# Mixer A's head columns stored from pairs of tiles, and the bias tables in 18 steps on GpSimd

## The chip, the cores and the metric

The kernel runs on 1 core of one Trainium2 chip. The metric is the device time of one execution in microseconds (us); the time before is the median of three runs. The profile is of one further execution of the same program on the same core.

## The reference

One layer of a hybrid decoder, batch 1, 2048 positions, width 1024, float32. What is computed, cut to what this case touches:

```
h    = rmsnorm(x, g_attn)
proj = h @ w_in + b_in                      # qa | ka | va | qb | kb | vb
qa, ka = rope(qa), rope(ka)                 # mixer A: 8 query heads, 2 key heads, 64 wide
oa   = banded attention(qa, ka, va), window 128, with sinks
ob   = dilated attention(qb, kb, vb), branches (128,1), (512,4), (2048,16),
       logits + rel_table[t5_bucket(distance)]        # one bias table per head of mixer B
x    = x + concat(rmsnorm(oa), rmsnorm(ob)) @ w_o
x    = x + SwiGLU feed-forward(rmsnorm(x));  return rmsnorm(x)
```

Each float32 product is made of three products of rounded halves: a tensor is split into a rounded high part and the remainder ("high and low").

## The kernel before

The program is built through a layer that puts the instructions of each engine into an order of its own: it takes the program as written, follows dependences and buffers, and may move an instruction ahead of others on its engine. Each engine then works its list strictly in order, so an instruction that waits holds all behind it. All loads and stores spoken of here go through the list of SyncE (SP) and one DMA queue.

Function `project` makes `h` (kept in SBUF as `hh`, `hl`) and v, and then works in two stages.

**The rotary stage** makes qa and ka. There are 20 tiles, numbered 0 to 19 here: for each block of 128 output columns, in the order c = 4 (the two key heads), 0, 1, 2, 3 (two query heads each), four tiles t = 0 to 3 of 512 positions. For one tile:

- `rotated`: `gemm` (L175) sums 24 matmuls into a PSUM buffer `acc` (pool `ps2`, 8 buffers). ScalarE (ACT) and VectorE (DVE) copy two quarters each, swapped, into `t1` (L297, L299); VectorE multiplies by cosine and sine (`t2`, L301; `t1`, L302); GpSimd (POOL) adds them into `t2` (L303). `t1` has 2 buffers, `t2` has 4.
- `parted`: ScalarE casts `t2` into the high part of `hia` (L312) and VectorE subtracts for the low part (L313). `hia` holds one column block of 2048 positions and has 1 buffer. It runs two tiles late: after tile n is rotated, tile n - 2 is parted. After t = 3 the block is stored by two DMAs of 1 MB (`store_heads`, L181): kA for c = 4, then four stores of qA. The next block's first cast can start only when that store has landed.
- The weights of the next block but one are loaded at t = 1 (`load_w`, L163, raw buffer 1) and split by ScalarE (L165) and VectorE (L167, `wl`).

**The bias tables** are made beside it, in the same loop, by the closure that `bias_tables` returns: after tiles 2 to 9 `rows(h)` for the 8 heads (one VectorE operation `lw`, L397, three matmuls `accb` into the same PSUM pool, L400, three ScalarE copies `lt`, L402, 2 buffers, three stores into the scratch `Ls`, L403), after tiles 10 to 17 `table(h)`: loads of `Ls` into `tt`, `n4` and four quarters of `n1` (L407, L409, L412; one buffer each), two VectorE copies that put them into `tt` (L413, L414), and a store of `tt` (L416, `Ts`). The layer brings many of these forward.

**The next stage** starts with tiles 20 to 23 of mixer B's projection (`proj_b`, first weights `C_QB`), whose results `hi` go out to qB, and then mixer A's attention units: logits `s` (L449) from `ka` and `qa`, which are loaded from the stored kA and qA (L549, L557). The list of SyncE holds the last qA store between the loads of `ka`.

Of the kernel before, what the change touches and what calls it, by code (L numbers as in the profile page):

```python
# [10 lines left out]
F32 = mybir.dt.float32  # L11
# [6 lines left out]
P = 128  # L18
# [3 lines left out]
NH = 8  # L22
# [125 lines left out]
def project(tc, es, ident, half, x, g_attn, w_in, b_in, sinks, rel, rope, mask_a, onehot, sc):  # L148
# [129 lines left out]
    with ExitStack() as ex:  # L278
# [27 lines left out]
        def parted(c, t, t2):  # L306

            if t == 0:
                his[c] = rp.tile([P, 2, S], F32R, tag="hi", name="hia", bufs=1)
            hi = his[c]  # L310
            hj = [hi[:, u].rearrange("p (j r a) -> p r j a", j=16, r=16)[:, 4 * t:4 * t + 4] for u in range(2)]
            nc.scalar.copy(hj[0], t2)  # L312
            nc.vector.tensor_sub(hj[1], t2, hj[0].bitcast(F32))  # L313
            if t == NT - 1:
                store_heads(sc.qA if c < 4 else sc.kA, 2 * c if c < 4 else 0, hi, slice(0, S))
# [4 lines left out]
        for n, (c, t) in enumerate(seq):  # L320
            t2 = rotated(c, t, w[c])
            if t == 1 and n + 3 < len(seq):
                cn = seq[n + 3][0]
                w[cn] = load_w(cn * P)
            behind.append((c, t, t2))
            if len(behind) > 2:
                parted(*behind.pop(0))
            if 0 <= n - 2 < 2 * NH:
                bias((n - 2) // NH, (n - 2) % NH)
# [4 lines left out]
    with ExitStack() as ex:  # L334
# [3 lines left out]
        w = {}  # L338

        def proj_b(todo, ps=ps, tag="mm"):  # L340
            for c0, c, t in todo:
                if t == 0:
                    w[c0] = load_w(c0 + c * P)
# [24 lines left out]
def bias_tables(tc, es, ps, rel, onehot, sc):  # L368
# [26 lines left out]
    def rows(h):  # L395
        lw = bw.tile([P, P], F32R, tag="lw", name="lw")
        nc.vector.tensor_scalar(out=lw, in0=ones, scalar1=rhi[:, h:h + 1].bitcast(F32), scalar2=None, op0=ALU.mult)  # L397
        for b in range(3):
            acc = ps.tile([P, 384], F32, tag="mm", name="accb")
            nc.tensor.matmul(acc, lw, ohr[:, b, :], start=True, stop=True)  # L400
            lt = bw.tile([P, 384], F32, tag="lt", name="lt")
            nc.scalar.copy(lt, acc)  # L402
            nc.sync.dma_start(sc.L[h, b], lt)  # L403

    def table(h):
# [7 lines left out]
        nc.vector.tensor_copy(tt[:, 128:384].rearrange("p (c i) -> p c i", c=4), n4.rearrange("p (i c) -> p c i", c=4))  # L413
        nc.vector.tensor_copy(tt[:, 384:640].rearrange("p (g c a) -> p g c a", g=4, c=4),  # L414
# [3 lines left out]
    return lambda step, h: (rows, table)[step](h)  # L418
# [898 lines left out]
```

## Time and profile before

| | |
|---|---|
| median of 3 runs | 2417.63 us (2417.11 to 2417.86) |
| the profiled execution's own time | 2418.66 us |
| its span in the trace | 2416.9 us |
| TensorE (PE) busy | 2295.9 us, 95% of the span |
| VectorE / ScalarE / GpSimd busy | 1601.3 / 1056.2 / 466.5 us |
| mean granted TensorE clock | 0.979 |
| rotary stage, first matmul to first logits of mixer A | 146.69 to 318.65 us |

The span runs from the first to the last instruction on the core; the execution's own time has some 1.8 us around it. A row of the timeline has the start, the time (in us), the engine, line, operation, output<-input and count, and in brackets how long the engine had sat idle and what ended that. In a row of a wait table stand who waited for whom, the total, how often, and the longest.

### The profile page before, as it was taken

What the parts mean: (1) busy time and instruction counts of PE and PEld (TensorE: products, weight loads), DVE (VectorE), ACT (ScalarE), POOL (GpSimd) and SP (SyncE); (2) the same over time, 40 slices, a digit from 0 to 9 for tenths busy, and PEclk for the clock granted to TensorE, in tenths of its full rate; (3) what the DMA queues carried; (4) which work ended last, traced back from release to release, by engine and by line L of the source; (5) the groups of instructions that cost most, each with busy time, mean ns of one, the idle gap of its engine ahead of it and who ended that gap; (6) DMA issues with size and microseconds to landing.
All of it is one profiled execution on the core that took longest, in us unless ns stands there. A gap on an engine that the chain in (4) does not pass through costs nothing.

```text
span 2416.9 us, 33849 instructions
## 1 busy us (share of the span) xinstructions
PE 2295.9 (95%) x11765; PEld 1953.6 (81%) x11765; DVE 1601.3 (66%) x3151; ACT 1056.2 (44%) x2371; POOL 466.5 (19%) x418
## 2 busy tenths in 40 slices
PE   7998799998999989897999999999999999999998
PEld 7986678887999878786788888778888878888887
DVE  5335644446999977658876776796676746657555
ACT  5323245553988873325323323342323325444442
POOL 2321211112111010014132332423232331000000
PEclk9998999998999989998999999999999999999999
DMA  7656576659898697855545444343233329768651
GB/s 220 211 172 195 142 190 177 165 143 258 203 221 211 166 269 193 257 165 193 195 152 175 160 150 166 123 143 101 96 114 100 105 82 397 263 195 290 201 191 70
DMA packets 280091, 436.20 MB, mean 180 GB/s; under 512 B 24224, under 2 KB 152864, under 8 KB 273136
## 3 DMA queue, kind: packets, MB, share of 16 engines
q1 hardware_dynamic: 273600, 419.21, 56.4%
q0 software_dynamic: 3728, 10.30, 1.5%
q10 hardware_dynamic: 2592, 4.52, 0.7%
q8 instruction: 93, 1.52, 0.3%
q14 instruction: 78, 0.64, 0.1%
HBM read 286.50 MB, written 147.46 MB: 180 GB/s over the span
## 4 chain that ended last, share of the span: by engine, by line
PE 51%; DVE 5%; DMA 3%; issue 1%; POOL 0%; ACT 0%; DVEq 0%; POOLq 0%; SPq 0%; ACTq 0%
PE bY L1245 7%; PE Yu L1051 7%; PE Yg L1051 6%; PE bZ L1245 5%; PE bX L1245 5%; PE Zu L1051 4%; PE Xu L1051 4%; PE Xg L1051 4%; PE Zg L1051 4%; PE acco L913 3%; DMA ob<-oB 1%; DVE wl L1018 1%; DMA ob<-oA 1%; DVE xs L935 1%; DMA hraw<-hT 0%
## 5 line engine op out<-in xcount | busy, mean ns | idle before, releaser
L1198 DVE TENSOR_TENSOR o<-r,o 128x1024 fp32r<-128x1024 f32 x154 | 190.5, 1243 | 133.0 <-ACT o L1197 124.6
L1197 ACT CAST o<-r 128x1024 fp32r<-128x1024 f32 x154 | 162.2, 1054 | 227.0 <-DMA r<-in_w_down_dram 61.2
L1016 ACT CAST wh<-T 128x512 fp32r<-128x512 f32 x176 | 107.6, 621 | 247.7 <-PE Yu L1051 78.9
L1145 POOL TENSOR_TENSOR c<-c,c 128x512 f32<-128x512 f32 x66 | 104.3, 1580 | 570.1 <-DVE c L1069 390.7
L496 DVE TENSOR_TENSOR hl<-pt,hl 128x512 fp32r<-128x512 f32 (+1 forms) x224 | 145.5, 657 | 78.4 <-ACT hl L495 77.5
L471 ACT ACTIVATE p<-t,m 128x256 f32<-128x256 f32 (+1 forms) x384 | 177.2, 479 | 16.2 <-DVE m L696 16.2
L175 PE MATMUL acc<-hh,wh 128*128 128x512 f32 x416 | 168.0, 404 | 14.8 <-DVE t L301 13.7
L1245 PE MATMUL bY<-o 128*128 128x512 f32 x792 | 180.5, 389 | 0.0
L1245 PEld LDWEIGHTS bY<-o 128*128 128x128 f32 x792 | 148.6, 188 | 30.9
L913 PE MATMUL acco<-woh,oT 128*128 128x512 f32 x512 | 163.6, 397 | 3.8 <-ACT oT L884 3.4
L175 PE MATMUL acc<-hh,wl 128*128 128x512 f32 x416 | 167.1, 402 | 0.0
L175 PE MATMUL acc<-hl,wh 128*128 128x512 f32 x416 | 166.7, 401 | 0.0
L1018 DVE TENSOR_TENSOR wl<-T,wh 128x512 fp32r<-128x512 f32 x176 | 155.1, 891 | 0.3
L514 PE MATMUL o<-hl,v 128*128 128x128 f32 (+1 forms) x816 | 140.7, 293 | 7.3 <-DVE hl L496 6.0
L495 ACT CAST hl<-pt 128x512 fp32r<-128x512 f32 (+1 forms) x224 | 125.2, 568 | 44.6 <-PE pt L490 43.9
L490 PE MATMUL pt<-ident,p 128*128 128x128 f32 x848 | 135.4, 283 | 3.9 <-DVE hl L496 2.1
L449 PE MATMUL s<-k,q 128*128 128x256 f32 (+1 forms) x768 | 122.5, 292 | 10.1 <-DVE nm L453 6.0
L1245 PE MATMUL bX<-o 128*128 128x512 f32 x528 | 120.6, 389 | 1.1 <-DVE o L1198 1.1
L514 PEld LDWEIGHTS o<-hl,v 128*128 128x128 f32 x816 | 111.3, 193 | 12.0 <-DVE hl L496 9.3
L1245 PE MATMUL bZ<-o 128*128 128x512 f32 x528 | 120.3, 389 | 0.0
L913 PEld LDWEIGHTS acco<-woh,oT 128*128 128x128 f32 x512 | 97.0, 190 | 25.6 <-ACT oT L884 4.1
L1245 PEld LDWEIGHTS bX<-o 128*128 128x128 f32 x528 | 99.0, 188 | 22.1 <-DVE o L1198 1.5
(465 smaller groups left out, 5803.6 us busy)
## 6 DMA issues: line engine op xcount, KB each, us to landing
r<-actS SPq DMA_DIRECT2D x154, 256.0 KB
actS<-c SPq DMA_DIRECT2D x128, 256.0 KB
wraw_g<-in_w_gate_dram SPq DMA_DIRECT2D x44, 512.0 KB
wraw_u<-in_w_up_dram SPq DMA_DIRECT2D x44, 512.0 KB
r<-wT SPq DMA_DIRECT2D x88, 256.0 KB
r<-in_w_down_dram SPq DMA_DIRECT2D x66, 256.0 KB
k<-kB SPq DMA_DIRECT2D x32, 512.0 KB
draw<-in_w_down_dram SPq DMA_DIRECT2D x22, 512.0 KB
```

Source lines behind the costliest of these rows:

```text
L175: nc.tensor.matmul(acc, a[:, k, :], h[t][:, k, :], start=(n == 0), stop=(n == 3 * KC - 1))
L471: nc.scalar.activation(b["pv"](p[:, i, :n]), b["tv"](b["t"]), AF.Exp, scale=-1.0, bias=nm[:, c:c + 1], accum_out=l[:, c:c + 1])
L490: nc.tensor.transpose(pt[:, sl, :], p[:, i, hfn * P:(hfn + 1) * P], ident)
L495: nc.scalar.copy(hi, pt[:, a:z, :])
L496: nc.vector.tensor_sub(lo, pt[:, a:z, :], hi.bitcast(F32))
L514: nc.tensor.matmul(out, v[:, vi, :], mov, start=(first and n == 1), stop=(last and n == 2 * len(jobs)))
L913: nc.tensor.matmul(acc, oT[kk // 2][:, kk % 2, a, i * P:(i + 1) * P], b[:, kk, :], start=(n == 0), stop=(n == 11))
L1018: nc.vector.tensor_sub(lo, src, hi.bitcast(F32))
L1051: nc.tensor.matmul(bank, a[:, k], b[:, k], start=(first and m == 0), stop=(m == 11), skip_group_check=not first)
L1197: nc.scalar.copy(o[:, 0], r)
L1198: V.tensor_sub(o[:, 1], r, o[:, 0].bitcast(F32))
L1245: nc.tensor.matmul(bank[i], o[:, u, 0, i * P:(i + 1) * P], o[:, v, 1, :], start=(first and j == 0 and m == 0), stop=(j == NP - 1 and m == ...
```

## The change

Three things, all in `project` and `bias_tables`:

- `parted` no longer follows two tiles behind. After a tile with t = 3 the block's tiles t = 0 and 1 are parted, after the next block's t = 0 its tiles t = 2 and 3. Both instructions are marked so that the layer keeps them where the program has them. What is left after tile 19 is parted at the end.
- The bias work is cut into 18 steps, one after each tile from 2 to 19: two pieces (one matmul, copy and store each) per step in the first 12, from step 2 on a `load(h)` in each even step and a `table(h)` in each odd one. The two copies into `tt` are on GpSimd.
- The weights of mixer B's first tile are loaded after tile 17, in the loop of the rotary stage.

```diff
-            nc.scalar.copy(hj[0], t2)
-            nc.vector.tensor_sub(hj[1], t2, hj[0].bitcast(F32))
+            tc.keep_in_program_order(nc.scalar.copy(hj[0], t2))
+            tc.keep_in_program_order(nc.vector.tensor_sub(hj[1], t2, hj[0].bitcast(F32)))
...
+            elif t == 1:
+                w_next = load_w(C_QB)
             behind.append((c, t, t2))
-            if len(behind) > 2:
-                parted(*behind.pop(0))
-            if 0 <= n - 2 < 2 * NH:
-                bias((n - 2) // NH, (n - 2) % NH)
+            if t in (0, 3):
+                for x_ in [x_ for x_ in behind if x_[1] in ((2, 3) if t == 0 else (0, 1))]:
+                    parted(*x_)
+                    del behind[[y[:2] for y in behind].index(x_[:2])]
+            if n >= 2:
+                bias(n - 2)
...
-        w = {}
+        w = {C_QB: w_next}
...
-                if t == 0:
+                if t == 0 and (c0, c) != (C_QB, 0):
                     w[c0] = load_w(c0 + c * P)
...
+    def piece(h, b):
+        if b == 0:
+            lws[h] = rows(h)
+        acc = ps.tile([P, 384], F32, tag="mm", name="accb")
+        nc.tensor.matmul(acc, lws[h], ohr[:, b, :], start=True, stop=True)
+        lt = bw.tile([P, 384], F32, tag="lt", name="lt")
+        nc.scalar.copy(lt, acc)
+        nc.sync.dma_start(sc.L[h, b], lt)
...
+    def table(h):
+        tt, n4, n1 = raws[h]
-        nc.vector.tensor_copy(tt[:, 128:384].rearrange("p (c i) -> p c i", c=4), n4.rearrange("p (i c) -> p c i", c=4))
-        nc.vector.tensor_copy(tt[:, 384:640].rearrange("p (g c a) -> p g c a", g=4, c=4),
+        nc.gpsimd.tensor_copy(tt[:, 128:384].rearrange("p (c i) -> p c i", c=4), n4.rearrange("p (i c) -> p c i", c=4))
+        nc.gpsimd.tensor_copy(tt[:, 384:640].rearrange("p (g c a) -> p g c a", g=4, c=4),
                               n1.rearrange("p (a c g) -> p g c a", g=4, c=4))
         nc.sync.dma_start(sc.T[h], tt)
...
+    def bias(step):
+        for n in (2 * step, 2 * step + 1):
+            if n < 3 * NH:
+                piece(n // 3, n % 3)
+        if step >= 2:
+            (table if step % 2 else load)(step // 2 - 1)
```

After the rotary stage, from tile 20 on, every engine's list is the same as before. Where the order moved, at three places:

ScalarE before, around the change from block c = 1 to c = 2 (tiles 12 and 13 of block 2 are t_2274 and t_2322, tiles 14 and 15 are t_2378 and t_2427; COPY t_ is L297 for the tile whose `t1` it names, in the order 12 to 17):

```order
L297 COPY t_2317<-acc 32x512 x2
L312 CAST hia<-t_2274 128x4x16x8
L312 CAST hia<-t_2322 128x4x16x8
L297 COPY t_2373<-acc 32x512 x2
L165 CAST wh_2667<-raw_2665 128x1024
L297 COPY t_2422<-acc 32x512
L312 CAST hia<-t_2378 128x4x16x8
L297 COPY t_2422<-acc 32x512
L297 COPY t_2470<-acc 32x512
L312 CAST hia<-t_2427 128x4x16x8
```

and ScalarE in the change, the same tiles (12 to 15 are t_2276, t_2337, t_2390, t_2433):

```order
L297 COPY t_2332<-acc 32x512 x2
L297 COPY t_2385<-acc 32x512 x2
L165 CAST wh_2530<-raw_2528 128x1024
L297 COPY t_2428<-acc 32x512 x2
L313 CAST hia<-t_2276 128x4x16x8
L313 CAST hia<-t_2337 128x4x16x8
L297 COPY t_2470<-acc 32x512 x2
L313 CAST hia<-t_2390 128x4x16x8
L313 CAST hia<-t_2433 128x4x16x8
```

The casts of a block's first two tiles, which wait for the store of the block before, moved behind the copies of its other two tiles; the casts of these follow one tile later.

GpSimd in the change, around tables 6 and 7 (L427, L428 are the copies; t_2276 to t_2475 are the additions of tiles 12 to 16; before, this list holds the additions alone):

```order
L303 TENSOR_TENSOR t_2276<-t_2276,t_2271 128x512
L427 COPY tt<-n_2487 128x256
L428 COPY tt<-n_2489 128x256
L303 TENSOR_TENSOR t_2337<-t_2337,t_2332 128x512
L303 TENSOR_TENSOR t_2390<-t_2390,t_2385 128x512
L427 COPY tt<-n_2573 128x256
L428 COPY tt<-n_2575 128x256
L303 TENSOR_TENSOR t_2433<-t_2433,t_2428 128x512
L303 TENSOR_TENSOR t_2475<-t_2475,t_2470 128x512
```

The addition of tile 15 now stands behind both copies of the last table.

SyncE in the change, from the store of block c = 1 to that of c = 2 (L413 stores pieces, L417, L419, L422 load the table, L430 stores it, raw_2999 are weights):

```order
L181 DMA qA<-hia 64x2x2048 x2
L413 DMA Ls<-lt 128x384 x2
L417 DMA tt<-Ls 128x128
L419 DMA n_2573<-Ls 128x1x256
L422 DMA n_2575<-Ls 32x1x256
L430 DMA Ts<-tt 128x640
L422 DMA n_2575<-Ls 32x1x256 x3
L417 DMA tt<-Ls 128x128
L163 DMA raw_2999<-in_w_in_dram 128x8x128
L430 DMA Ts<-tt 128x640
L581 DMA qa<-qA 128x2x512 x2
L181 DMA qA<-hia 64x2x2048 x2
```

The last table's loads stand behind the store of block 1, and two loads of `qa` (L581, 512 KB each) directly ahead of the store of block 2; before, there was one table less behind that store.

## Rows read from the trace of the kernel before

**Rows 1.** Busy time of each engine by stretch of the span: the stretch and its length, then busy us and instructions of PE, PEld, DVE, ACT and POOL, the granted share of TensorE's clock, the DMA share and GB/s.

```profile
188.00:213.00 25.00, 17.76 (x52) 13.45 (x53) 13.96 (x23) 10.15 (x19) 3.85 (x3) 0.73 0.73 197
213.00:274.00 61.00, 61.00 (x272) 50.64 (x271) 34.65 (x52) 19.21 (x34) 11.85 (x8) 1.00 0.67 184
274.00:319.00 45.00, 26.68 (x102) 21.02 (x101) 19.15 (x28) 10.91 (x18) 7.88 (x5) 0.85 0.60 143
319.00:560.00 241.00, 239.51 (x1399) 209.83 (x1399) 112.82 (x334) 131.72 (x359) 34.68 (x56) 0.99 0.61 167
```

**Rows 2.** Waits of PE between 150 and 340 us: who waited for whom, us in total, times, the longest.

```profile
PE acc L175 <- DVE t L301: 13.7, 2, 10.0
PE accb L400 <- ACT lt L402: 6.5, 3, 2.5
PE s L449 <- DMA ka<-kA: 4.6, 1, 4.6
```

**Rows 3.** Timeline of PE: the first matmul of tiles 0, 19, 20 and 22, and the first logits.

```profile
146.69 0.50 PE L175 MATMUL acc<-hh,wh 128*128 128x512 f32 x1 [0.65 <-DVE vt L245]
...
268.75 0.39 PE L175 MATMUL acc<-hh,wh 128*128 128x512 f32 x1
...
284.39 0.80 PE L175 MATMUL acc<-hh,wh 128*128 128x512 f32 x1 [10.04 <-DVE t L301]
...
301.18 0.50 PE L175 MATMUL acc<-hh,wh 128*128 128x512 f32 x1 [3.67 <-DVE t L301]
...
318.65 1.35 PE L449 MATMUL s<-ka,qa 128*128 128x128 f32 x7 [4.60 <-DMA ka<-kA]
```

**Rows 4.** Timeline of the DMA issues of SyncE: the five stores of a column block (kA, then four of qA), and the two loads of `qa`.

```profile
187.62 1.33 SPq L181 DMA_DIRECT2D kA<-hia  x2
...
222.03 1.48 SPq L181 DMA_DIRECT2D qA<-hia  x2
...
253.24 1.27 SPq L181 DMA_DIRECT2D qA<-hia  x2
...
267.16 2.37 SPq L557 DMA_DIRECT2D qa<-qA  x2
...
279.43 1.29 SPq L181 DMA_DIRECT2D qA<-hia  x2
...
305.68 1.27 SPq L181 DMA_DIRECT2D qA<-hia  x2
```

**Rows 5.** Timeline of ACT: the four casts that a store had held.

```profile
200.60 0.62 ACT L312 CAST hia<-t 128x512 fp32r<-128x512 f32 x1 [6.76 <-DMA kA<-hia]
...
234.87 1.15 ACT L312 CAST hia<-t 128x512 fp32r<-128x512 f32 x2 [6.29 <-DMA qA<-hia]
...
265.40 1.14 ACT L312 CAST hia<-t 128x512 fp32r<-128x512 f32 x2 [6.66 <-DMA qA<-hia]
...
291.27 1.14 ACT L312 CAST hia<-t 128x512 fp32r<-128x512 f32 x2 [7.71 <-DMA qA<-hia]
```

**Rows 6.** Waits of DVE and of ACT between 150 and 340 us (columns as in rows 2).

```profile
DVE hia L313 <- ACT hia L312: 21.7, 6, 6.2
...
DVE tt L414 <- DMA n<-Ls: 10.9, 5, 5.5
...
DVE tt L413 <- DMA Ts<-tt: 5.8, 4, 2.9
...
ACT lt L402 <- DMA Ls<-lt: 23.5, 11, 5.5
```

**Rows 7.** Timeline of DVE: the first product (L301) of tiles 15, 16 and 17, where nothing but the work itself holds a tile; and a subtraction for the low part (L313).

```profile
275.16 0.75 DVE L301 SCALAR_TENSOR_TENSOR t<-acc,bcol,tab 128x512 f32<-128x512 f32 x1
...
278.71 0.69 DVE L313 TENSOR_TENSOR hia<-t,hia 128x512 fp32r<-128x512 f32 x1
279.43 0.75 DVE L301 SCALAR_TENSOR_TENSOR t<-acc,bcol,tab 128x512 f32<-128x512 f32 x1
...
283.59 0.75 DVE L301 SCALAR_TENSOR_TENSOR t<-acc,bcol,tab 128x512 f32<-128x512 f32 x1 [0.64 <-ACT t L297]
```

**Rows 8.** Round trips over DRAM, from the timelines of SyncE, ACT and DVE, in order of time: a store of two pieces and the copy that waited for its buffer; a table's store and the load that waited for it; the last quarter of `n1` and the copy that read it.

```profile
186.20 0.88 SPq L403 DMA_DIRECT2D Ls<-lt  x2
...
188.44 0.48 ACT L402 COPY lt<-accb 128x384 f32<-128x384 f32 x1 [1.02 <-DMA Ls<-lt]
...
210.75 0.31 SPq L416 DMA_DIRECT2D Ts<-tt  x1
...
213.70 0.43 SPq L407 DMA_DIRECT2D tt<-Ls  x1
...
240.96 0.61 SPq L412 DMA_DIRECT2D n<-Ls  x1
...
243.96 0.38 DVE L414 COPY tt<-n 128x256 f32<-128x256 f32 x1
```

**Rows 9.** GpSimd and VectorE at the same moment, from their timelines, in order of time: an addition, a table copy of VectorE that started beside it, and an addition with a split of weights beside it.

```profile
240.64 1.29 POOL L303 TENSOR_TENSOR t<-t,t 128x512 f32<-128x512 f32 x1 [9.16 <-DVE t L302]
240.67 1.52 DVE L413 COPY tt<-n 128x256 f32<-128x256 f32 x1 [0.20 <-DMA Ts<-tt]
...
270.92 2.83 POOL L303 TENSOR_TENSOR t<-t,t 128x512 f32<-128x512 f32 x1 [9.29 <-DVE t L302]
271.40 1.20 DVE L167 TENSOR_TENSOR wl<-raw,wh 128x1024 fp32r<-128x1024 f32 x1
```

More of the change, by code (lines that the diff above doesn't have):

```diff
@@ L397, in rows, with load @@
         nc.vector.tensor_scalar(out=lw, in0=ones, scalar1=rhi[:, h:h + 1].bitcast(F32), scalar2=None, op0=ALU.mult)
[L398 to L405, printed above, removed]
+        return lw
+    def piece(h, b):
[6 more added lines that the diff above has]
+        nc.sync.dma_start(sc.L[h, b], lt)
+    def load(h):
         tt = bw.tile([P, 640], F32, tag="tt", name="tt", bufs=1)
@@ L412, in table @@
             nc.sync.dma_start(n1[g * 32:(g + 1) * 32], skew(h, 2, [(4, 4), (16, 8)], 127 + (W - 1) * g, 2 * P))
-        nc.vector.tensor_copy(tt[:, 128:384].rearrange("p (c i) -> p c i", c=4), n4.rearrange("p (i c) -> p c i", c=4))
-        nc.vector.tensor_copy(tt[:, 384:640].rearrange("p (g c a) -> p g c a", g=4, c=4),
+        raws[h] = tt, n4, n1
+    def table(h):
+        tt, n4, n1 = raws[h]
+        nc.gpsimd.tensor_copy(tt[:, 128:384].rearrange("p (c i) -> p c i", c=4), n4.rearrange("p (i c) -> p c i", c=4))
+        nc.gpsimd.tensor_copy(tt[:, 384:640].rearrange("p (g c a) -> p g c a", g=4, c=4),
                               n1.rearrange("p (a c g) -> p g c a", g=4, c=4))
         nc.sync.dma_start(sc.T[h], tt)
-    return lambda step, h: (rows, table)[step](h)
+    lws, raws = {}, {}
+    def bias(step):
[4 more added lines that the diff above has]
+            (table if step % 2 else load)(step // 2 - 1)
+    return bias
 ident_f = lambda ap: ap
```

## The prediction

> **What bounds the kernel now.** I read the stretches first. From 213 to 274 us and from 319 us on TensorE has no gap; the change touches the stage up to 319 us alone, so what this stage gives back comes off the whole, and that is the first thing to see [rows 1]. The stage's losses lie in two stretches: from 188 to 213 us TensorE is busy for 17.8 of 25 us at a granted clock of 0.73, from 274 to 319 for 26.7 of 45 us at 0.85 [rows 1]. Of its two levels, 1.2 and 2.4 GHz, the lower thus fills a good part of the first stretch, after each of the short stalls there.
>
> Next the waits of TensorE: it waits for buffers that VectorE has not yet emptied (13.7 us), for bias pieces that ScalarE has not emptied (6.5), and at the end for `ka` (4.6) [rows 2]. In the timeline tile 20 starts 10.04 us late, tile 22 3.67 us late, and the first logits come at 318.65 [rows 3]. TensorE is therefore the one that is held.
>
> Then who holds VectorE and ScalarE. VectorE loses 21.7 us to casts into `hia` and 10.9 + 5.8 us to the tables' loads and stores; ScalarE loses 23.5 us to the two `lt` buffers [rows 6]. Neither is short of work time: where nothing holds them a tile takes 4.2 us (275.16, 279.43, 283.59) [rows 7], against 5.4 us of TensorE (24 of the 272 matmuls in 61 us [rows 1]).
>
> Last, what the casts wait for. Each of the five stores of 2 MB keeps its successor's casts out until it has landed: 187.62 to 200.60, 222.03 to 234.87, 253.24 to 265.40, 279.43 to 291.27, that is 13.0, 12.8, 12.2 and 11.8 us [rows 4, 5]. From landing to the next store go another 21.4, 18.4, 14.0 and 14.4 us [rows 4, 5]. From the fifth store at 305.68 to the logits it is 13.0 us [rows 3, 4]. **The stage is this chain: store, landing, the tiles still to be done, next store.**
>
> **The change, part by part.**
>
> *Pairs.* Before, a landed store is followed by the casts of two tiles, and then by the copies and products of about three tiles before the next store can go. With pairs, while a store is under way, ScalarE and VectorE do tiles t = 1 to 3 of the next block, whose `t2` fit into the four buffers; after landing come two casts, one tile, two casts. So tiles move from behind a landing into its shadow. How many depends on what else stops ScalarE in that shadow.
>
> *Pieces.* What stops it is `lt`. In the order, ScalarE reaches the pieces of tile 6 behind the kA store, and those of tile 10 behind the first qA store; their buffers come free only when piece stores queued behind the 2 MB have landed. So in the first two intervals two tiles remain after landing, later one, and for the last block none.
>
> The first interval after landing: a piece copy 0.48, its store's round trip of 2.2 us (issued at 186.20, buffer free at 188.44), two more copies 1.0 [rows 8]; two tiles at 4.2, 8.4; two subtractions at 0.69, 1.4 [rows 7]; then SyncE issues four loads of the next tables ahead of the store, 2.6 (0.61 each) [rows 8]. Sum 16.1, against 21.4: **5.3 gained**. The second has a cast of weights more, about 1.1, and a load less: 16.5, against 18.4: **1.9 gained**.
>
> *Tables on GpSimd.* The third interval holds table 7. Its loads stand behind the store, and the addition of tile 15 stands behind its copies, and the next store needs tile 15. After landing: the load of `n4`, a quarter of `n1` and the table store, 1.5; three quarters of `n1`, 1.9; their landing, 2.4 (240.96 + 0.61 to 243.96) [rows 8]; one copy; an addition 1.29 [rows 9]; a cast 0.6 and a subtraction 0.7 [rows 5, 7]. No row has this copy on GpSimd. From below it is VectorE's 0.38 [rows 8], from above the slowest addition, 2.83 [rows 9]; nearest is the undisturbed addition, 1.29 for twice the columns and two inputs, and I take 0.8. Sum 9.2, against 14.0: **4.8 gained**. Tile 16 runs beside it.
>
> *The last interval.* All four casts of block 3 come after landing, with the tiles done: four casts at 0.6 and a subtraction, 3.1, against 14.4: **11.3 gained**. But the two `qa` loads, 1 MB, which stood 12 us ahead of the store before (267.16 against 279.43 [rows 4]), and the weights now stand directly ahead of it. At the store's own rate 1 MB takes 5.9 us; some of it is over when the store is issued. I charge 4.5, with 0 and 5.9 as ends.
>
> *Collisions.* An addition beside VectorE's two-input subtraction of weights took 2.83 instead of 1.29, and a VectorE copy beside an addition 1.52 instead of 0.38 [rows 9]. This happened twice here in a stretch without other long operations; 16 more GpSimd operations come. I charge one collision on the chain, 1.5.
>
> *Weights.* `C_QB` earlier is worth nothing by itself: its split ended at 272.6 (271.40 + 1.20 [rows 9]) while tile 20 started at 284.39 for another reason [rows 3]. With the rest it is needed at about 275 and comes with tile 15, so it costs nothing either.
>
> *TensorE.* It must not become the later one. Tile 15's addition ends some 12 us earlier than before, at about 266.4 (the third qA store at 279.43 - 5.3 - 1.9 - 4.8 = 267.4, less a cast and a subtraction beside other work). Tile 17 needs its `t1` buffer, and tile 20 needs tile 18's PSUM buffer, so tile 20 starts at 266.4 + 2 x 4.2 = 275; four tiles of 5.4 and 2.3 us at the lower clock (what tiles 20 and 21 took over 10.8 us: 284.39 to 301.18 less 3.67 [rows 3]) end at 299. The logits by the chain: 318.65 - 5.3 - 1.9 - 4.8 - 11.3 + 4.5 + 1.5 = 301.4. So the chain still rules, by 2 us, and the gain is 17.3. First store: kept at 187.62, since in the new order it follows the loads of table 1 where it followed parts of them before.
>
> 2418.66 - 17.3 = 2401.4 for the profiled execution, which is 1.0 above the median of the runs; **2400.4 us** for the median.
>
> **Weighing a rule.** The rows of the collision say that one of the two engines waited for the other to finish. The Trainium skill, "SBUF — State Buffer", section "SBUF: two separate sides", states that VectorE and GpSimd share one port pair, locked for a whole instruction by whoever starts first, against VectorE operations with two SBUF inputs or in a two-port mode. That speaks against moving copies to GpSimd beside L302 and L314, which have two such inputs; the trace agrees with it twice (2.83 and 1.52 us). By it nearly every copy on the chain would collide, which is rival 2; by my one collision the sum is as above.
>
> **Rivals.**
>
> 1. *More: `lt` does not hold.* If piece stores slip in ahead of the 2 MB, the first two intervals keep one tile each: 4.2 + 2.2 more, twice, 12.8. Against it stand 23.5 us of waits for `lt` [rows 6]. Time 2388.
> 2. *Collisions at each copy.* Of the copies, six lie between a landing and the next store (of tables 2 to 5 and 7); at 2.83 - 1.29 = 1.5 each [rows 9] this costs 9.2 in place of 1.5: gain 9.6, time 2408.
> 3. *The wait moves, and nothing is left.* VectorE's 10.9 + 5.8 = 16.7 us of waits for table loads [rows 6] go to GpSimd, whose additions stand behind the copies. If all of it falls between landing and store, the 17.3 are gone: time 2417. For it: additions 4, 10, 12, 13 and 15 stand behind copies. Against: an addition may lag two tiles before `t1` runs out.
> 4. *Slower: the copies themselves.* If a strided copy on GpSimd takes far longer than an addition, it is the gate. Six lie on the chain, so from (17.3 / 6) + 0.8 = 3.7 us each the change loses, and at 5 us each the time is 2417.63 - 17.3 + 6 x 4.2 = 2426. For it: no row has such a copy. Against: the longest GpSimd operation here, disturbed, is 2.83.
>
> That the layer undoes the order is no rival: the order shows casts, copies and loads where the program puts them.
>
> **How the numbers follow.** Forecast 0.50, rival 1 0.10, rival 2 0.14, rival 3 0.13, rival 4 0.13. A measurement of this kernel tells 0.2%, 4.8 us, from no change. The first three are faster by more: 0.74. Rival 3 is within: 0.13. Rival 4 is slower: 0.13. The copy at its ends moves the forecast by 6 x 0.4 down and 6 x 2.0 up, the `qa` loads by 4.5 down and 1.4 up: 2393.5 to 2414. The range takes rival 1 with 2 us to spare, 2386, and reaches to 2416 for part of rival 3; left out are rival 4, half of rival 3's near side and a tail below, about 0.2.
>
> **What would show it.** The stores at about 187.6, 216, 245, 267 and 288 us, and the logits at 300 to 302; between landing and next store about 16, 16.5, 9 and 3 us in place of 21.4, 18.4, 14.0 and 14.4; no wait of tile 20 near 10 us; VectorE's wait for `hia` under 10 us. GpSimd has 16 copies of 0.5 to 1.3 us and idles on `n` loads instead of VectorE. I am wrong in the chain if the stores keep their old distances, in the copy if it is over 3 us, in the queue if the last store lands over 18 us after its issue, and in the carry-over if the logits come early and the rest of the span grows.

## The result

| | before | after |
|---|---|---|
| median, first measurement | 2417.74 us (4 runs) | 2399.76 us (4 runs, 2396.47 to 2408.14) |
| median, measured again beside the experiments | 2418.99 us (17 runs) | 2400.28 us (5 runs, 2399.21 to 2407.07) |
| ratio after/before, first and again | | 0.993 (0.9904 to 0.9956), 0.9919 (0.9906 to 0.9931) |

The change makes the kernel 18 to 19 us faster, 0.7 to 0.8%. The forecast was 2400.4. The size came out; how the stage gets to it did not. As the terms below show, that the sum fits is luck: errors of nearly 10 us in each direction cancel.

The same changed program was profiled twice: in an execution of 2408.14 us and in one of 2399.21 us. The stage differs by 1.5 us between them (logits 156.22 and 154.67 us after the first matmul of tile 0). The other 7.4 us lie outside it: the first execution enters the stage 2.3 us later, and what follows its logits takes 5.1 us longer. The rows here are of the second execution, which is near the median.

**The profile after.** The four stretches of [rows 1]:

```profile
188.00:213.00 25.00, 25.00 (x114) 20.89 (x113) 12.26 (x17) 9.70 (x18) 5.60 (x6) 1.00 0.63 184
213.00:274.00 61.00, 49.74 (x209) 40.25 (x207) 39.80 (x50) 20.93 (x37) 20.08 (x18) 0.94 0.68 185
274.00:319.00 45.00, 41.14 (x199) 34.83 (x200) 22.72 (x54) 18.49 (x45) 6.69 (x5) 0.92 0.84 215
319.00:560.00 241.00, 235.23 (x1388) 206.42 (x1386) 113.90 (x332) 130.18 (x354) 37.11 (x60) 0.99 0.63 177
```

The two stretches that were thin are now filled: 25.0 of 25 us at a clock of 1.00 in place of 17.8 at 0.73, and 41.1 of 45 us in place of 26.7. In the middle one TensorE is now busy for 11 us less: part of the idle time has moved there.

The waits of TensorE between 150 and 340 us, and its timeline at tiles 0 and 20 and the first logits, as in [rows 2, 3]:

```profile
PE acc L175 <- DVE t L301: 8.3, 1, 8.3
PE accb L410 <- ACT lt L412: 6.5, 1, 6.5
```

```profile
146.55 0.50 PE L175 MATMUL acc<-hh,wh 128*128 128x512 f32 x1 [0.65 <-DVE vt L245]
...
277.86 0.80 PE L175 MATMUL acc<-hh,wh 128*128 128x512 f32 x1 [8.28 <-DVE t L301]
...
301.22 1.12 PE L473 MATMUL s<-ka,qa 128*128 128x128 f32 x8
```

The logits come 154.67 us after the first matmul of tile 0, in the kernel before 171.96: 17.3 us sooner. They no longer wait for `ka`. What stands ahead of them is TensorE's own work on tiles 20 to 23, which began with a wait of 8.28 us at tile 20. (Before, one of the eight matmuls of these logits comes already at 313.83; 318.65 is where the other seven start, behind their wait for `ka`. The times of the kernel before are counted to 318.65.)

The five stores and the `qa` loads on SyncE, and what ScalarE does when each of the first four has landed, as in [rows 4, 5] (the row at 268.45 is the cast that waits for tile 15's addition):

```profile
182.23 1.30 SPq L181 DMA_DIRECT2D kA<-hia  x2
...
214.77 1.27 SPq L181 DMA_DIRECT2D qA<-hia  x2
...
246.88 1.27 SPq L181 DMA_DIRECT2D qA<-hia  x2
...
267.61 3.20 SPq L581 DMA_DIRECT2D qa<-qA  x2
270.91 1.30 SPq L181 DMA_DIRECT2D qA<-hia  x2
...
287.02 1.27 SPq L181 DMA_DIRECT2D qA<-hia  x2
```

```profile
195.47 0.96 ACT L412 COPY lt<-accb 128x384 f32<-128x384 f32 x2 [6.31 <-DMA Ls<-lt]
...
227.95 0.99 ACT L412 COPY lt<-accb 128x384 f32<-128x384 f32 x2 [6.21 <-DMA Ls<-lt]
...
259.52 1.15 ACT L313 CAST hia<-t 128x512 fp32r<-128x512 f32 x2 [1.80 <-DMA qA<-hia]
...
268.45 0.62 ACT L313 CAST hia<-t 128x512 fp32r<-128x512 f32 x1 [3.66 <-POOL t L303]
...
283.18 2.19 ACT L313 CAST hia<-t 128x512 fp32r<-128x512 f32 x4 [1.53 <-DMA qA<-hia]
```

After the first two stores ScalarE is held by `lt`, as the prediction said; after the third and fourth it comes to the casts 1.5 to 1.8 us ahead of the landing. From landing to next store it is 19.3, 18.9, 11.4 and 3.8 us, where it was 21.4, 18.4, 14.0 and 14.4. (The first two landings are taken from the piece store behind the 2 MB, whose end frees `lt`.)

The waits of VectorE, ScalarE and GpSimd in that stretch, as in [rows 6]:

```profile
POOL tt L427 <- DMA Ts<-tt: 23.8, 5, 8.9
ACT lt L412 <- DMA Ls<-lt: 21.9, 7, 6.3
...
DVE wl L167 <- ACT wh L165: 14.0, 3, 6.0
POOL tt L427 <- DMA n<-Ls: 14.0, 2, 9.2
...
POOL tt L428 <- DMA n<-Ls: 10.4, 6, 4.3
...
DVE hia L314 <- ACT hia L313: 4.2, 3, 2.5
```

VectorE's 21.7 us for `hia` are 4.2, and its 16.7 us for the tables are gone: GpSimd now has 48.2 us of them. New is VectorE's wait of 14.0 us for `wh`, the rounded weights: twice its split of weights stands in its list at a place where ScalarE is itself held by `lt`.

### The profile page after: what moved, and what is told of

Read it like the earlier page. It is cut to its first block, busy times and chain, and to the rows that moved or that the text cites. A ratio compares the mean times of both kernels' runs of the same rounds, so it can differ in the third digit from the quotient of the medians.

```text
span 2405.9 us, 33862 instructions
## 1 busy us (share of the span) xinstructions
PE 2294.8 (95%) x11765; PEld 1957.2 (81%) x11765; DVE 1604.3 (67%) x3135; ACT 1057.5 (44%) x2371; POOL 481.4 (20%) x434
## 4 chain that ended last, share of the span: by engine, by line
PE 51%; DVE 5%; DMA 3%; issue 1%; POOL 0%; ACT 0%; SPq 0%; DVEq 0%; POOLq 0%; ACTq 0%
PE bY L1269 7%; PE Yu L1075 7%; PE Yg L1075 6%; PE bZ L1269 5%; PE bX L1269 5%; PE Zu L1075 4%; PE Xu L1075 4%; PE Xg L1075 4%; PE Zg L1075 4%; PE acco L937 3%; DVE wl L1042 1%; DMA hraw<-hT 1%; DMA ob<-oB 1%; DVE xs L959 1%; DMA draw<-in_w_down_dram 0%
## 5 line engine op out<-in xcount | busy, mean ns | idle before, releaser
L495 ACT ACTIVATE p<-t,m 128x256 f32<-128x256 f32 (+1 forms) x384 | 178.7, 488 | 18.4 <-DVE m L720 18.4
L538 PEld LDWEIGHTS o<-hl,v 128*128 128x128 f32 x816 | 113.9, 197 | 11.3 <-DVE hl L520 10.0
L473 PEld LDWEIGHTS s<-k,q 128*128 128x128 f32 x768 | 106.4, 203 | 15.1 <-DVE nm L477 4.9
L477 DVE CUSTOM_DVE_ANT_0 t<-s,tab 128x256 f32<-128x256 f32 (+1 forms) x344 | 112.9, 369 | 8.6 <-PE s L473 5.4
```

The lines of the kernel that those rows point to most:

```text
L473: nc.tensor.matmul(s[:, i, :n], b["q"], b["k"][m], start=(m == 0), stop=(m == 1))
L495: nc.scalar.activation(b["pv"](p[:, i, :n]), b["tv"](b["t"]), AF.Exp, scale=-1.0, bias=nm[:, c:c + 1], accum_out=l[:, c:c + 1])
L538: nc.tensor.matmul(out, v[:, vi, :], mov, start=(first and n == 1), stop=(last and n == 2 * len(jobs)))
```

## The experiments

For each run the table has the steps of the chain, in us: the first store (kA, called K) after tile 0's first matmul, the four distances from store to store (the four qA stores are called Q0 to Q3, so that Q1 is the second and Q2 the third), and from the last store to the logits; the logits after tile 0; and the wait of tile 20. They come from the profiled execution of each, the medians from all their runs, the ratios from runs of the kernel before on the same chip (medians 2418.6 to 2419.7). The last two distances of t7_pin, t7_actq and pin_actq go by the first half of the last store. In before, pairs_only, pairs_pool and gp_twice one matmul of the logits comes 4.8 to 11.1 us ahead of the rest, which wait for `ka`; the table goes by the rest. The profiled executions lie within 4.1 us of their medians, except that of pairs_only: it took 2421.97 us, 11.7 above its median. Its stage is 9.3 us shorter than before all the same; what it lost lies outside the stage.

| run | kA | K to Q0 | Q0 to Q1 | Q1 to Q2 | Q2 to Q3 | Q3 to logits | logits | tile 20 waits | median | ratio to before |
|---|---|---|---|---|---|---|---|---|---|---|
| before | 40.93 | 34.41 | 31.21 | 26.19 | 26.25 | 12.97 | 171.96 | 10.0 | | |
| again (the change) | 35.68 | 32.54 | 32.11 | 24.03 | 16.11 | 14.20 | 154.67 | 8.3 | 2400.28 | 0.9919 (0.9906 to 0.9931) |
| pairs_only | 41.10 | 36.22 | 34.00 | 21.62 | 16.77 | 12.99 | 162.70 | none | 2410.27 | 0.9968 (0.9956 to 0.998) |
| bias_only | 34.55 | 30.52 | 33.38 | 26.25 | 26.15 | 13.62 | 164.47 | 17.6 | 2413.80 | 0.9969 (0.9957 to 0.9981) |
| no_pin | 35.67 | 30.49 | 33.13 | 26.46 | 26.07 | 14.11 | 165.93 | 16.9 | 2411.87 | 0.9971 (0.996 to 0.9981) |
| pairs_pool | 40.97 | 34.70 | 30.55 | 21.49 | 16.80 | 12.99 | 157.50 | none | 2404.51 | 0.9938 (0.9923 to 0.9954) |
| dve_copies | 40.16 | 33.89 | 32.63 | 31.02 | 16.80 | 15.06 | 169.56 | 19.5 | 2411.94 | 0.997 (0.996 to 0.998) |
| late_w | 36.53 | 32.48 | 32.24 | 24.25 | 16.46 | 14.23 | 156.19 | 7.9 | 2401.41 | 0.9926 (0.9907 to 0.9946) |
| gp_twice | 38.17 | 29.97 | 30.27 | 27.40 | 19.86 | 12.97 | 158.64 | 7.4 | 2405.56 | 0.9943 (0.9927 to 0.9958) |
| t7_pin | 36.33 | 32.73 | 31.70 | 21.03 | 17.37 | 16.57 | 155.73 | 5.7 | 2402.78 | 0.9925 (0.9907 to 0.9942) |
| lt_actq | 38.43 | 29.86 | 31.13 | 21.58 | 16.80 | 15.01 | 152.81 | 12.0 | 2396.00 | 0.9892 (0.9877 to 0.9906) |
| t7_actq | 38.10 | 29.47 | 30.37 | 21.02 | 17.36 | 16.92 | 153.24 | 8.9 | 2398.51 | 0.9914 (0.99 to 0.9929) |
| pin_actq | 37.84 | 27.64 | 27.94 | 23.25 | 23.11 | 16.93 | 156.71 | 8.9 | 2401.40 | 0.9929 (0.9913 to 0.9946) |

**The change itself, beside the others.** No edit.

> The change as it is, on the chip of the next three kernels. Expected 2400 us, 17 to 18 below the kernel before, with logits between 301 and 305 us.

Measured 2400.28, 18.7 below, logits at 301.22. As expected.

**The pairs alone.** The kernel before with this edit:

```diff
-            nc.scalar.copy(hj[0], t2)
-            nc.vector.tensor_sub(hj[1], t2, hj[0].bitcast(F32))
+            tc.keep_in_program_order(nc.scalar.copy(hj[0], t2))
+            tc.keep_in_program_order(nc.vector.tensor_sub(hj[1], t2, hj[0].bitcast(F32)))
...
-            if len(behind) > 2:
-                parted(*behind.pop(0))
+            if t in (0, 3):
+                for x_ in [x_ for x_ in behind if x_[1] in ((2, 3) if t == 0 else (0, 1))]:
+                    parted(*x_)
+                    del behind[[y[:2] for y in behind].index(x_[:2])]
```

> The kernel before with the pairs alone (both instructions kept in the order of the program); bias tables by head with their copies on VectorE, and mixer B's first weights, as before. Chain theory: the last two intervals from landing to store are the pairs' own (about 9 and 4.5 us in place of 14.0 and 14.4), the first two stay at 18 to 21 since three pieces per head hold ScalarE: some 14 us gained, 2404. Rival, the bias steps carry the gain (VectorE freed of its 16.7 us of waits for tables): 2412 or more. Rival, neither part does anything alone: 2417.

Measured 2410.27, 8.7 gained, between the first theory and its rival. The place is right: the last two distances fall by 14.1 us. But the first two do not stay, they grow by 4.6. The logits wait for `ka`, as before, and TensorE is done 10 us ahead of them:

```profile
311.89 1.83 PE L451 MATMUL s<-ka,qa 128*128 128x128 f32 x7 [10.12 <-DMA ka<-kA]
```

Part of the growth is a collision that the pairs bring with them. The subtraction for the low part on VectorE, by line, in this run (last columns: busy us, mean ns, idle before), where there is no copy on GpSimd:

```profile
L313 DVE TENSOR_TENSOR hia<-t,hia 128x512 fp32r<-128x512 f32 x20 | 20.7, 1069 | 0.0
```

Alone it takes 0.69 us [rows 7].

**The bias work alone.** The changed kernel with the old two lines of `parted` and its old place:

```diff
-            tc.keep_in_program_order(nc.scalar.copy(hj[0], t2))
-            tc.keep_in_program_order(nc.vector.tensor_sub(hj[1], t2, hj[0].bitcast(F32)))
+            nc.scalar.copy(hj[0], t2)
+            nc.vector.tensor_sub(hj[1], t2, hj[0].bitcast(F32))
...
-            if t in (0, 3):
-                for x_ in [x_ for x_ in behind if x_[1] in ((2, 3) if t == 0 else (0, 1))]:
-                    parted(*x_)
-                    del behind[[y[:2] for y in behind].index(x_[:2])]
+            if len(behind) > 2:
+                parted(*behind.pop(0))
```

> The change without the pairs: 18 steps, copies on GpSimd, first weights early, but the casts two tiles behind and not held in the program's order. Chain theory: about two tiles still follow every landing, the last interval stays at 13 to 14 us, at most 5 us gained from tables off VectorE: 2413 to 2418. Rival, the bias steps carry the gain: 2405 or less.

Measured 2413.80, 5.2 gained. The last two distances are those of before to 0.1 us; what is gained is 6.4 us up to the first store and 3.9 in the first distance, of which the second gives 2.2 back. The same subtraction here, with 16 copies on GpSimd and no pairs:

```profile
L314 DVE TENSOR_TENSOR hia<-t,hia 128x512 fp32r<-128x512 f32 x20 | 14.5, 733 | 38.0 <-ACT hia L313 37.8
```

733 ns against 1069: the copies hardly touch it, the pairs do. The product L302, which also has two inputs in SBUF, takes 803 ns in the mean here and 743 with the pairs and no copies, so there too the copies cost little, 1.2 us over all 20 tiles.

**The pairs without the hold on their order.** The change with the first two `+` lines of the pairs undone.

> The change with casts and subtractions of the pairs not held in the order of the program; in this order the casts of a block's first two tiles stand again ahead of the copies of the tiles behind them. Theory (the gain is a tile or two moved into the shadow of each store): ScalarE's waits for kA and qA come back at 6 to 8 us each, the time is that of the change without pairs, 2411 to 2416. Rival, the pairs matter by their place in the program only: 2400.

Measured 2411.87, and from the first store on every step is that of the bias work alone to 0.5 us. The layer puts the casts ahead again, and ScalarE stands before the landing:

```profile
258.21 1.14 ACT L313 CAST hia<-t 128x512 fp32r<-128x512 f32 x2 [10.04 <-DMA qA<-hia]
```

So the pairs are worth nothing by their place in the program; it is the order of ScalarE's list that counts.

**Pairs and GpSimd, without the 18 steps.** The pairs alone, and `nc.gpsimd.tensor_copy` in `table`.

> Pairs as in the change and the tables' copies on GpSimd, but the bias work by head as in the kernel before (three pieces after each of tiles 2 to 9, a table after each of 10 to 17) and mixer B's first weights late. Theory, pairs pay when VectorE does not wait for tables, and the 18 steps add little: 2400 to 2405. Rival, the steps are needed, since three pieces per tile hold ScalarE at the first two stores: 2408 to 2411, as with the pairs alone.

Measured 2404.51, 14.1 gained, as expected; the 18 steps are worth the other 4.6, and the intervals of the two ratios overlap. Against the change the first store is 5.3 us later and the next four distances are 1.3 us shorter together. Here it is `ka` that the logits wait for, 10.93 us, and tile 20 waits for nothing. The last copy of table 7 runs while the second qA store (issued at 255.23) is still under way:

```profile
257.06 0.63 POOL L416 COPY tt<-n 128x256 f32<-128x256 f32 x1 [0.81 <-DMA n<-Ls]
```

In the change it comes 7.0 us after the landing of that store. So the steps bring the first store forward and put the last table behind a store that it was ahead of.

**The steps and the pairs, without GpSimd.**

```diff
-        nc.gpsimd.tensor_copy(tt[:, 128:384]...
-        nc.gpsimd.tensor_copy(tt[:, 384:640]...
+        nc.vector.tensor_copy(tt[:, 128:384]...
+        nc.vector.tensor_copy(tt[:, 384:640]...
```

> The change with the tables' 16 copies on VectorE instead of GpSimd, the 18 steps, pairs and weights as in the change. Theory: VectorE waits for the table loads that stand behind a 2-MB store, some 10 to 17 us in all, and its tiles with it: half of that lies between a landing and the next store, 2405 to 2409. Rival (collisions and GpSimd waits cost as much as they save): 2400 or below.

Measured 2411.94, worse than expected: of the 18.7 us that the change gains 7.7 are left. VectorE and TensorE between 150 and 340 us:

```profile
DVE tt L427 <- DMA n<-Ls: 21.8, 4, 10.5
PE acc L175 <- DVE t L301: 19.8, 2, 19.4
```

The two longest waits of VectorE for a table, in its timeline:

```profile
205.75 0.39 DVE L427 COPY tt<-n 128x256 f32<-128x256 f32 x1 [10.52 <-DMA n<-Ls]
...
270.68 0.39 DVE L427 COPY tt<-n 128x256 f32<-128x256 f32 x1 [8.44 <-DMA n<-Ls]
```

The first stands behind the kA store (issued at 186.82), the second behind the second qA store (253.34): VectorE waits for a table load that has to pass 2 MB, while with the pairs it would have had tiles to do. So the parts need each other: with the copies on VectorE the pairs gain 8.7 us and with the steps 7.7, with the copies on GpSimd 14.1 and 18.7. Steps and copies without the pairs gain 5.2; the copies on GpSimd alone were not tried.

**Mixer B's first weights late.** The edits on `C_QB` undone.

> The change without the early load of mixer B's first weights (loaded where the kernel before loads them). Prediction's term: worth nothing, 2400, tile 20 starts at the same time and its weights are split before. Rival, the weights come after tile 20's buffer is free and hold it: 2402 to 2408.

Measured 2401.41, not to be told from the change. Worth nothing, as predicted.

**Each GpSimd copy twice.**

> The change with each of the tables' GpSimd copies done twice (16 more of 0.63 us). Theory, only table 7's two copies lie on the path to tile 20 and to the third qA store: 1.3 us and a collision more at most, 2400 to 2403. Rival 2 of the prediction, a collision for each copy on the chain: up to 9 us more, 2409. Rival 4, GpSimd's copies are the gate: six copies of 0.63 on the chain, 4 us more and above.

Measured 2405.56, 14.1 gained where the change gains 18.7, and no theory holds as it stands. The third distance grows by 3.4 us: table 6's loads, too, stand behind Q1 in this order, so that table 7's first copy comes 23.0 us after Q1's issue in place of 18.4, and two more copies, 1.2 us, stand ahead of tile 15's addition; against that, the `qa` loads no longer stand ahead of the third qA store. The fourth grows by 3.8 us for a reason of its own, and the first two shrink. VectorE in this run:

```profile
207.83 1.29 DVE L314 TENSOR_TENSOR hia<-t,hia 128x512 fp32r<-128x512 f32 x2
...
213.14 1.29 DVE L314 TENSOR_TENSOR hia<-t,hia 128x512 fp32r<-128x512 f32 x2
...
292.62 0.17 DVE L554 TENSOR_SCALAR nsnk<-snk 128x8 f32<-128x8 f32 x1 [4.56 <-DMA snk<-in_sinks_dram]
```

In the first distance GpSimd's additions stand behind more copies and start only at 209.58 and 215.48, when each pair has ended; both pairs run undisturbed at 1.29 us, where they took 2.83 and 2.38 in the change, and the distance is 2.57 us shorter. At the end VectorE waits 4.56 us for the sinks, 8 numbers in each of 128 rows, whose load stands behind the third qA store and the `qa` loads in this order; the last subtraction, and so the last store, stand behind it.

**The last table's copies behind the additions.** `keep` is `tc.keep_in_program_order` for the last head, and nothing for the others:

```diff
+        keep = tc.keep_in_program_order if h == NH - 1 else (lambda i: i)
-        nc.gpsimd.tensor_copy(tt[:, 128:384]...
-        nc.gpsimd.tensor_copy(tt[:, 384:640]...
+        keep(nc.gpsimd.tensor_copy(tt[:, 128:384]...)
+        keep(nc.gpsimd.tensor_copy(tt[:, 384:640]...)
```

> The change with the two GpSimd copies of the last table (7) kept in the order of the program, that is behind the additions of tiles 16 to 19 instead of ahead of that of tile 15; all else the same code. Theory (after the change TensorE's wait of 8.3 us ahead of tile 20 rules, and it comes from tile 15's addition behind table 7's copies, which wait for loads behind the store Q1): tile 15's addition runs about 8 us sooner, the wait of tile 20 falls under 3 us, the third qA store follows Q1's landing by 6 to 7 us in place of 11.4. The logits then come up to 6 us sooner, 2394, if the two qa loads, which this order puts behind the last store, do not hold them; if they do, 2400. Rival, the wait of tile 20 comes from VectorE's and ScalarE's own work: it stays over 6 us and the time stays at 2400.

Measured 2402.78. The first half of the theory holds, that tile 15's addition runs sooner; the second, that tile 20's wait falls under 3 us, doesn't, and the rival is nearer. In the change the addition of tile 15 stands behind table 7, whose load stands behind Q1; GpSimd and VectorE there:

```profile
265.29 0.79 POOL L427 COPY tt<-n 128x256 f32<-128x256 f32 x1 [7.75 <-DMA Ts<-tt]
266.53 0.63 POOL L428 COPY tt<-n 128x256 f32<-128x256 f32 x1 [0.46 <-DMA n<-Ls]
267.12 2.54 POOL L303 TENSOR_TENSOR t<-t,t 128x512 f32<-128x512 f32 x2
...
277.06 0.75 DVE L301 SCALAR_TENSOR_TENSOR t<-acc,bcol,tab 128x512 f32<-128x512 f32 x1 [0.64 <-ACT t L297]
```

and here GpSimd, VectorE and TensorE, in order of time:

```profile
258.90 1.30 POOL L303 TENSOR_TENSOR t<-t,t 128x512 f32<-128x512 f32 x1 [1.77 <-DVE t L302]
...
265.37 2.38 DVE L314 TENSOR_TENSOR hia<-t,hia 128x512 fp32r<-128x512 f32 x2
...
274.61 0.75 DVE L301 SCALAR_TENSOR_TENSOR t<-acc,bcol,tab 128x512 f32<-128x512 f32 x1 [0.64 <-ACT t L297]
...
275.41 0.79 PE L175 MATMUL acc<-hh,wh 128*128 128x512 f32 x1 [5.70 <-DVE t L301]
...
301.72 1.23 PE L474 MATMUL s<-ka,qa 128*128 128x128 f32 x8 [1.66 <-DMA qa<-qA]
```

Counted from each run's tile 0 (145.99 here, 146.55 in the change), the addition runs 7.7 us sooner, yet tile 20 starts only 1.9 us sooner and still waits 5.7. The rest is VectorE's and ScalarE's own list: after Q1 lands come a pair, tile 16, a pair (2.38 us, a collision), tile 17 and tile 18's product, one behind the other. The distance to the third qA store is 3.0 us shorter (21.03 against 24.03), yet the logits come 1.1 us later: in this order the `qa` loads stand behind the last store and hold them for 1.66 us, and tiles 20 to 23 take 24.65 us in place of 23.36, at a granted clock of 0.89 in place of 0.93.

**The pieces on another DMA queue.**

```diff
-        nc.sync.dma_start(sc.L[h, b], lt)
+        nc.scalar.dma_start(sc.L[h, b], lt)
```

> The change with the piece stores (into Ls) on ScalarE's own DMA queue, so that they do not stand behind a 2-MB store in SyncE's. Chain theory: ScalarE's waits for lt of 6.3 us behind the first two stores go, two tiles move into their shadow, the first two intervals from landing to store fall from 19 to about 13 us each and the logits by 12: 2388. Rival, the two queues share the DMA engines and the pieces land no sooner: 2400, the waits for lt as long. Rival, another path holds tile 20 by then (PSUM buffers emptied behind table 7): the stores come sooner, the logits by 5 us at most: 2395.

Measured 2396.00, 4.3 below the change, the fastest here, though the intervals of the ratios touch. The third of the three expectations has the size. ScalarE's waits for `lt` fall from 21.9 to 13.4 us in all, not to nothing, and a new one comes, as its timeline shows (ACTq is its own DMA issue):

```profile
183.09 5.21 ACTq L413 DMA_DIRECT2D Ls<-lt  x2
188.35 0.58 ACT L297 COPY t<-acc 32x512 f32<-32x512 f32 x1 [4.90 <-DMA n<-Ls]
...
195.04 0.48 ACT L412 COPY lt<-accb 128x384 f32<-128x384 f32 x1 [4.27 <-DMA Ls<-lt]
```

ScalarE stood for 4.90 us behind two issues that took 5.21, while SyncE was issuing table loads (two issues at 176.93 took 0.91). The four distances are 5.4 us shorter together and the first store is 2.8 later, so the last store comes 2.7 sooner, and tile 20, at 128.6 us after tile 0, as well. The logits gain 1.9 us in this execution; it took 2399.47 us, no less than that of the change (2399.21), so the 4.3 us of the medians do not show in it.

**Both, and all copies behind.** t7_actq is the last two together; pin_actq holds all tables' copies in the order of the program.

> The change with the last table's copies kept behind tile 19 and the piece stores on ScalarE's DMA queue, both as tried alone. Theory, each takes a wait from the same end (Q1's landing sooner, tile 20's wait smaller): 2393 to 2396. Rival, the loads of qa behind the last store now hold the logits: 2396 to 2400, with a wait for qa of 2 to 5 us.

> As the run before, but all tables' copies kept in the order of the program, each two tiles later than the layer puts them. Theory: no addition stands behind a copy that waits for loads behind a store, GpSimd's waits no longer reach the tiles, the first store goes ahead of table 1's loads: 2391 to 2396. Rival, the loads of qa behind the last store hold the logits: 2396 to 2400.

Measured 2398.51 and 2401.40: the rival in both, in the second 1.4 us above its range. The `qa` loads behind the last store hold the logits for 2.06 us in the first. In the second, TensorE and VectorE, in order of time:

```profile
269.06 0.80 PE L175 MATMUL acc<-hh,wh 128*128 128x512 f32 x1 [8.92 <-DVE t L301]
...
285.55 0.17 DVE L551 TENSOR_SCALAR nsnk<-snk 128x8 f32<-128x8 f32 x1 [6.62 <-DMA snk<-in_sinks_dram]
...
303.27 2.07 PE L473 MATMUL s<-ka,qa 128*128 128x128 f32 x8 [9.56 <-DMA qa<-qA]
```

Tile 20 starts 122.5 us after tile 0, 8.8 sooner than in the change, and all of it is lost again in a wait of 9.56 us: VectorE waits 6.62 us for the sinks ahead of the last subtraction, so the last store is late, and the `qa` loads, which stand behind it, are later. A version that loads both early was not tried.

## Why the prediction was right, point by point

The time was right, and its sum was right to the tenth: 17.3 us were predicted for the stage and 17.3 found in the second execution (15.7 in the first). Its terms were not: 5.3 us came from a place that was put at nothing and 3.0 from a charge that was too high, and four intervals were worked out too short. The errors of the table's rows add up to 9.8 us in either direction; that these cancel is luck. Before and after, in us gained:

| term | predicted | measured |
|---|---|---|
| first store | 0 | 5.3 |
| first interval after landing | 5.3 | 2.1 |
| second | 1.9 | -0.6 |
| third | 4.8 | 2.6 |
| last | 11.3 | 10.6 |
| `qa` loads ahead of the third qA store, and the landings | -4.5 | -1.5 |
| collisions | -1.5 | in the intervals |
| from the last store to the logits | 0 | -1.2 |

**What bounds the kernel** was read rightly for the kernel before, not for the change. The chain of stores sets the end before and in pairs_only, pairs_pool and gp_twice, where the logits wait 4.6 to 10.9 us for `ka`. In the change, and in bias_only, no_pin, dve_copies, late_w and lt_actq, they wait for no load and come when TensorE is through tiles 20 to 23, which tile 20's wait has delayed. The logits after tile 0 order the runs nearly as the medians do. dve_copies is the exception, with 2.4 us gained there and 7.7 by the medians: its profiled execution is 2.8 above its median and that of the kernel before 1.0 below the median that it is compared with, and 1.6 us lie outside the stage.

**The first store** is the step that failed most. The prediction kept it, from the order of SyncE alone. What it waits for is the block of tiles ahead of it, and there VectorE and ScalarE of the kernel before were held, in order of time:

```profile
173.98 0.39 DVE L413 COPY tt<-n 128x256 f32<-128x256 f32 x1 [2.43 <-DMA n<-Ls]
...
182.98 0.39 DVE L414 COPY tt<-n 128x256 f32<-128x256 f32 x1 [3.69 <-DMA n<-Ls]
...
185.82 0.48 ACT L402 COPY lt<-accb 128x384 f32<-128x384 f32 x1 [5.50 <-DMA Ls<-lt]
```

The first two, VectorE's waits for tables, go with the copies to GpSimd; the third, ScalarE's wait for `lt`, goes with two pieces per tile in place of three. Undoing either brings the store back to 40 to 41 us (dve_copies 40.16, pairs_pool 40.97); undoing the pairs does not (34.55). So it takes both: one alone gains 0.8 us at most. VectorE's 16.7 us for tables were in [rows 6]; the prediction used them only in rival 3, against the change.

**Pairs and pieces.** Two tiles behind the first two landings, one behind the third and none behind the last: as predicted. The first interval was 3.2 us longer than worked out (19.3 against 16.1). Two things were mis-sized: ahead of the two tiles ScalarE waits for `lt` twice more, 1.10 and 2.77 us, where one round trip of 2.2 was charged, and splits weights (1.05), which was charged to the second interval alone, 3.1 us more in all; and both pairs collide. VectorE and GpSimd, one pair undisturbed, and one with the addition beside it:

```profile
180.91 1.29 DVE L314 TENSOR_TENSOR hia<-t,hia 128x512 fp32r<-128x512 f32 x2
...
205.51 2.83 DVE L314 TENSOR_TENSOR hia<-t,hia 128x512 fp32r<-128x512 f32 x2
...
206.05 1.74 POOL L303 TENSOR_TENSOR t<-t,t 128x512 f32<-128x512 f32 x1
```

The two pairs of this interval take 2.83 and 2.38 in place of 1.29, 2.6 us, and the second interval has the same two. The four loads of SyncE, charged with 2.6, cost nothing: they were issued while VectorE worked. 3.1 and 2.6 more and 2.6 less are the 3.2.

**Tables on GpSimd.** The copies take 0.65 and 0.74 us in the mean, the longest 1.09, against 0.8 taken: rival 4 (3.7 and more) is out. The third interval was worked out step by step, and the copies start within 0.1 us of it; the two copies are 1.9 us with a wait between them where one of 0.8 was counted, and the cast, the subtraction and the issue of the `qa` loads another 1.2.

**The queue.** The third qA store lands 12.3 us after its issue with the two `qa` loads ahead of it, and after 11.8 without them close ahead, in t7_pin and in the kernel before [rows 4, 5]: 0.5 us, not 4.5. In bias_only, with the same loads 3.4 us ahead, it is 11.7. The lower end of the range, 0, was nearer.

**Collisions.** One was charged, 1.5 us; some four of 1.1 to 1.5 lie on the chain. (The trace of the kernel before had more than the two that were counted: another addition took 2.80 us at 296.16.) Rival 2 had the price and the wrong partner: it counted the copies. The subtraction takes 1069 ns in the mean with pairs and no copies, 733 with copies and no pairs. The cause is that a pair stands right behind VectorE's last product of a tile, at the moment when GpSimd adds that tile; where the additions come later, the pairs take 1.29 us again (gp_twice). The Trainium skill, "SBUF — State Buffer", section "SBUF: two separate sides", says that a VectorE operation with two SBUF inputs, which this subtraction has, and a GpSimd operation that reads SBUF exclude each other: the one that starts first keeps the ports that they share for its whole instruction, and the other waits. The trace agrees that one waits for the other: a pair and an addition are 1.29 us each alone, 2.6 one behind the other, and the pairs took 2.38 and 2.83 with the addition among them. It does not show that the first to start goes first: in [rows 9] the addition of 2.83 us begins at 270.92, ahead of the split at 271.40, and is the one that waits. The rule did speak against this change, though against the pairs, not the copies.

**Rival 1**, that `lt` does not hold, was wrong, with 21.9 us of waits for it. **Rival 3**, that the wait moves to GpSimd: it moved, all 48.2 us, and little of it reaches the chain, since an addition may lag. Where it does reach, at tile 15, it costs the distance to the third qA store 3.0 us (t7_pin).

**TensorE.** The prediction let the chain rule by 2 us and tile 20 start at 275 without a wait near 10. It starts at 277.86 after 8.28 us, its four tiles take 23.4, and they end last: 12.97 us after the last store, as before, would have been 300.0, and the logits come at 301.22. The chain of stores and the way over the PSUM buffers to tile 20 both hang on the landing of Q1, through tile 15's addition behind table 7, and lie within 2 us of each other. In t7_pin, lt_actq and t7_actq both end sooner after tile 0, tile 20's wait by 1.9, 2.7 and 4.7 us, the last store by 1.3, 2.7 and 4.2. Little of it is left at the logits: tiles 20 to 23 take 24.2 to 24.7 us there at a granted clock of 0.89 to 0.90 (0.93 in the change), and in the first and the third the `qa` loads hold the logits as well.

**Weights**: nothing, as said (late_w).

## What to carry to other kernels

Ask of each wait that goes away not only what it holds late in a chain, but also whether it holds the chain's first step: the gain of 5.3 us at the first store was in waits that had been read. Two parts of a change can need each other: pairs give VectorE work to do in the shadow of a store (while it is under way), and that was worth less where VectorE's list had a wait for a load behind that store (7.7 and 8.7 us against 14.1 and 18.7). When a chain has been shortened, look which load the new order puts behind a large store, however small: the sinks or `qa` held the end for 1.7 to 9.6 us in four of these runs. And a sum that comes out is no proof of its terms: here only the rows of the profile after showed that they were wrong.

## What was not expected of the hardware

Moving small stores to ScalarE's queue did not make them free for ScalarE: in lt_actq two issues took 5.21 us while SyncE was issuing too, and ScalarE stood for 4.90 of them. Two loads of 512 KB issued 3.3 us ahead of a 2-MB store in the same queue delayed its landing by 0.5 us at most (12.3 against 11.8, and 11.7 in bias_only). A strided copy of 128x256 float32 took GpSimd 0.63 us undisturbed, half of the 1.28 of an addition of 128x512.
